# Stick-breaking attention with tokens on the partitions, running sums on VectorE and four panels ahead of each norm

## The chip, the cores and the metric

The kernel runs on one core of a Trainium2 chip. The metric is the device time of one execution in microseconds (us); the time shown is the median of three runs. The engines are named as in the profile: PE is TensorE, DVE VectorE, ACT ScalarE, POOL GpSimd, SP SyncE (here it only issues transfers).

## The reference

One inference step of an encoder with two layers, in fp32, for 256 prompt tokens and 64 tokens of a running stream ("samples"), which the kernel carries together as T = 320 columns. The model dimension is 2048 (16 tiles of 128), the feed-forward one 8192.

```python
# layer 0                                     # layer 1
h = x @ w_in_a                                kv = x @ w_kv; h = x @ w_in_b
main = gate_b * short_conv(gate_c * xin)      main = stick_breaking(q, k, v)        # 12 heads of 128
# both
mix = concat(main, mem_attend(q_m, mem_k, mem_v)) @ w_out     # 4 memory heads, 256 memory tokens
x = layer_norm(ALPHA * x + mix, g0, b0)
x = layer_norm(ALPHA * x + square(relu(x @ w_ff1)) @ w_ff2, g1, b1)
# stick_breaking, strictly causal: keys s before query t
z = q . k / sqrt(128)
A[t, s] = exp(log_sigmoid(z[t, s]) + sum over s < j < t of log_sigmoid(-z[t, j]))
out[t] = sum over s of A[t, s] * v[s]
# mem_k, mem_v = memory tokens @ w_mem_kv, per layer
```

A prompt query sees the prompt's 256 tokens; a sample query sees 512 cached tokens and the 64 new ones.

## The kernel before

Products are kept at fp32 accuracy by splitting: ACT casts a chunk of weights (128x1024, 512 KB from SP's queue) to fp32r, `hi` (L135), DVE subtracts it from the chunk and leaves the rest, `lo` (L136), and `gemm` makes three products per tile of the inner dimension: lo with xh, hi with xl, hi with xh (L181 to L183). Activations lie with the model dimension on the partitions and the 320 tokens as columns. A panel is 256 output columns of weights, two tiles; it has 2 x 16 x 3 = 96 products. Three buffers hold raw chunks, five hi and lo; four PSUM banks (`pacc`) hold accumulators, four more (`paux`: zs, zp, tp, av) all else.

Work between panels is put into the stream of products by hand: `later(gap, fn)` queues a stage, and `tick`, called every 12 products, starts the next one when its gap is over. A scheduler then orders each engine's instructions by when their inputs are ready.

- `mem_kv` projects the memory tokens to keys and values for both layers at the start. It makes layer 0's K and V together, with K's accumulators in `pacc` and V's in `paux`; then layer 1's K and after it layer 1's V (L213 to L215), each in `pacc`. ACT copies finished accumulators to SBUF (L219, L223).
- Layer 1's projection gives for each of the 12 heads kT, qT and vT, a tile of 96 / 2 = 48 products each, so two heads are 288 products. Behind them `stick_z` makes the scores with the keys on the partitions, adds masks by a bf16 product with an identity, and forms softplus(z) by Abs, Exp, Ln on ACT and a maximum and addition on DVE (L626). `sums` adds the suffix sums on PE, as products of a triangle `ntri` with the split softplus (L660 to L665), straight onto the scores in PSUM; ACT's Exp gives the weights, and `values` multiplies them with v (L672 to L681). Sample scores and values are products of half the array's columns (L615, L679, L681).
- `Norm` gathers the residual `res` tile by tile (`add`), subtracts an early estimate of the mean (`center`), sums tiles and squares, and in `finish` gets mean and variance over the partitions by four fp32 products with a matrix of 1/2048 (L411 to L414). The next projection does not wait for it: its first two panels run on the not yet normalised xh, xl with two more columns (322), which carry the weight's sums with gain and bias, and `finished` repairs their results on DVE. `normalise`, called after every chunk step, makes the normalised `res` and its split in turns 2 to 5 (`AFTER`). The last norm writes the output instead (`write`): an addition and a multiplication per tile on DVE or POOL, gain and bias on ACT or DVE, then the transfer.

Of the kernel before, what the change touches and what calls it, by code (L numbers as in the profile page):

```python
# [10 lines left out]
F32 = mybir.dt.float32  # L11
# [6 lines left out]
P = 128  # L18
# [11 lines left out]
CK = 4  # L30
NKC = KT // CK
AFTER = (2, 3, 4, 5)
# [9 lines left out]
def encoder_step(  # L42
# [40 lines left out]
    with tc.tile_pool(name="early", bufs=1) as early:  # L83
# [3 lines left out]
        for _ in range(EARLY):  # L87
# [8 lines left out]
    ident_b = const.tile([P, P], BF16, name="ident_b")  # L96
    nc.vector.tensor_copy(ident_b, ident)

    mask_b = const.tile([P, P], BF16, name="mask_b")
    nc.gpsimd.memset(mask_b, 0.0)  # L100
    nc.gpsimd.affine_select(out=mask_b, in_=mask_b, pattern=[[1, P]], compare_op=ALU.is_gt,
                            fill=BIG, base=0, channel_multiplier=-1)
    ones = const.tile([P, P], F32, name="ones")
    nc.vector.memset(ones, -1.0)
    nones = const.tile([P, P], F32R, name="nones")
    nc.vector.tensor_copy(nones, ones)

    trif = res[:, KT - 1, :P]
    nc.gpsimd.memset(trif, -1.0)
    nc.gpsimd.affine_select(out=trif, in_=trif, pattern=[[-1, P]], compare_op=ALU.is_ge,  # L110
                            fill=0.0, base=0, channel_multiplier=1)
    ntri = const.tile([P, P], F32R, name="ntri")
    nc.vector.tensor_copy(ntri, trif)
    onesm = const.tile([P, P], F32, name="onesm")
    nc.vector.memset(onesm, 1.0 / DM)
    onesq = const.tile([P, P], F32, name="onesq")
    nc.vector.memset(onesq, 1.0 / (4 * P))
# [73 lines left out]
    def mem_kv(layer, whats, between=None, first=None):  # L191

        accs = {}
        for what in whats:
            for i in range(4):
                accs[what, i] = (pacc.tile([P, 512], F32, name="acc") if what == whats[0] else
                                 paux.tile([P, 512], F32, name=("zs", "zp", "tp", "av")[i]))[:, :NM]
        parts = [(what, part) for what in whats for part in range(2)]

        def products(c, what, part, wh, wl, ks):  # L200
            for j in range(2):
                acc = accs[what, 2 * part + j]
                cols = slice(j * P, (j + 1) * P)
                for k in ks:
                    kt = c * CK + k
                    mh, ml = memh[:, kt, :], meml[:, kt, :]
                    start, stop = kt == 0, kt == KT - 1
                    if what == 0:
                        mm(acc, lhsT=wl[:, k, cols], rhs=mh, start=start, stop=False)  # L209
                        mm(acc, lhsT=wh[:, k, cols], rhs=ml, start=False, stop=False)  # L210
                        mm(acc, lhsT=wh[:, k, cols], rhs=mh, start=False, stop=stop)
                    else:
                        mm(acc, lhsT=ml[:, cols], rhs=wh[:, k, :], start=start, stop=False)  # L213
                        mm(acc, lhsT=mh[:, cols], rhs=wl[:, k, :], start=False, stop=False)  # L214
                        mm(acc, lhsT=mh[:, cols], rhs=wh[:, k, :], start=False, stop=stop)  # L215
# [122 lines left out]
    class Norm:  # L338
# [3 lines left out]
        def __init__(self, idx, factor, last=False):  # L342
            self.idx, self.factor, self.last, self.turn = idx, factor, last, 0
            if not last:
# [7 lines left out]
        def ahead(self, m):  # L352
            if self.last:
                return
            r, g, hi = res[:, m, :], lg[:, self.idx, m:m + 1], xh[:, m, :T]
# [4 lines left out]
        def add(self, m, acc):  # L360
# [12 lines left out]
            if not last:  # L373
# [6 lines left out]
        def center(self):  # L380
# [8 lines left out]
            mm(cp, lhsT=onesq, rhs=self.s1, start=True, stop=True)  # L389
            c = work.tile([P, T], F32, name="cen", bufs=1)  # L390
            nc.scalar.copy(c, cp)
# [15 lines left out]

        def finish(self, sq):
            m1 = paux.tile([P, 512], F32, name="zp")[:, :T]
            m2 = paux.tile([P, 512], F32, name="zs")[:, :T]  # L410
            mm(m1, lhsT=onesm, rhs=self.s1, start=True, stop=False)  # L411
            mm(m2, lhsT=onesm, rhs=self.s2, start=True, stop=False)
            mm(m1, lhsT=onesm, rhs=res[:, KT - 1, :], start=False, stop=True)
            mm(m2, lhsT=onesm, rhs=sq, start=False, stop=True)  # L414
            msq = work.tile([P, T], F32, name="msq", bufs=1)
            nc.scalar.activation(msq, m1, AF.Square)
            nc.scalar.mul(mneg, m1, -1.0)
# [10 lines left out]
            if self.last:  # L428
                self.write()

        def write(self):

            for m in range(KT):
                r, g, b = res[:, m, :], lg[:, self.idx, m:m + 1], lb[:, self.idx, m:m + 1]
                engine = nc.gpsimd if m % 3 == 2 else nc.vector
                engine.tensor_tensor(out=r, in0=r, in1=mneg, op=ALU.add)  # L436
                engine.tensor_tensor(out=r, in0=r, in1=rstd, op=ALU.mult)  # L437
                if m % 4 == 3:
                    nc.vector.tensor_scalar(out=r, in0=r, scalar1=g, scalar2=b, op0=ALU.mult, op1=ALU.add)
                else:  # L440
                    nc.scalar.activation(r, r, AF.Identity, bias=b, scale=g)
                if m < 2:
                    nc.sync.dma_start(out=y_out[:, m, :], in_=r)
                elif m % 2:
                    nc.sync.dma_start(out=y_out[:, m - 1:m + 1, :], in_=res[:, m - 1:m + 1, :])

        def normalise(self, _):

            self.turn += 1
            if self.turn not in AFTER:  # L450
                return
            c = AFTER.index(self.turn)
            s = slice(c * CK, (c + 1) * CK)
            r = res[:, s, :]
            nc.vector.tensor_tensor(out=r, in0=r, in1=mneg.unsqueeze(1).to_broadcast([P, CK, T]), op=ALU.add)
            nc.vector.tensor_tensor(out=r, in0=r, in1=rstd.unsqueeze(1).to_broadcast([P, CK, T]), op=ALU.mult)
            for m in range(c * CK, (c + 1) * CK):
                nc.scalar.activation(res[:, m, :], res[:, m, :], AF.Identity, bias=lb[:, self.idx, m:m + 1],
                                     scale=lg[:, self.idx, m:m + 1])
            split(xh[:, s, :T], xl[:, s, :T], r)  # L460
# [18 lines left out]
    def feed_forward(layer, before):  # L479
        for g in range(4):  # L480
# [21 lines left out]
            for p in range(0, 8, 2):  # L502
                first = g == 0 and p == 0
                gemm([[w_ff1[layer, 8 * g + p + i, c] for c in range(NKC)] for i in range(2)], xh, xl,
                     lambda i, j, acc, p=p: hidden(2 * (p + i) + j, acc),
                     width=T + 2 if first else T, after=before.normalise if g == 0 else None)
# [88 lines left out]

    def stick_z(h, d):
        kT, qT = d["kT"], d["qT"]
        ckT = work.tile([P, PAST], F32, name="ckT")
        nc.gpsimd.dma_start(out=ckT, in_=ck[h])

        def z():

            d["zp"] = zp = paux.tile([P, 512], F32, name="zp")[:, :3 * P]
            d["zs"] = zs = paux.tile([P, 512], F32, name="zs")[:, :5 * TS]
            mm(zp[:, 0:P], lhsT=ident_b, rhs=mask_b, start=True, stop=False, **kw)
            mm(zp[:, P:2 * P], lhsT=ident_b, rhs=mask_b, start=False, stop=False, **kw)
            mm(zp[:, 0:P], lhsT=kT[:, 0:P], rhs=qT[:, 0:P], start=False, stop=True, **kw)
            mm(zp[:, P:2 * P], lhsT=kT[:, P:TP], rhs=qT[:, P:TP], start=False, stop=True, **kw)
            mm(zp[:, 2 * P:], lhsT=kT[:, 0:P], rhs=qT[:, P:TP], start=False, stop=True, **kw)
            qs = qT[:, TP:T]  # L610
            mm(zs[:, 4 * TS:], lhsT=ident_b, rhs=mask_b[:, 0:TS], start=True, stop=False, **kw)
            mm(zs[0:TS, 4 * TS:], lhsT=kT[:, TP:T], rhs=qs, start=False, stop=True, **kw)
            for b in range(4):
                for f in range(2):
                    mm(zs[f * 64:(f + 1) * 64, b * TS:(b + 1) * TS], lhsT=ckT[:, b * P + f * 64:b * P + (f + 1) * 64],  # L615
                       rhs=qs, start=False, stop=True, **kw)

            d["npr"] = npr = work.tile([P, 3 * P], F32, name="npr", bufs=1)
# [167 lines left out]
```

## Time and profile before

| | before |
|---|---|
| median of 3 runs (lowest, highest) | 2814.73 us (2813.58, 2815.86) |
| the profiled execution | 2817.14 us, its span 2815.4 us |
| busy PE / DVE / ACT / POOL | 2787.8 / 1427.9 / 1120.1 / 49.2 us |
| bytes moved | 427.52 MB, 152 GB/s over the span |

Busy time of an engine is the time in which it had an instruction running; products on PE overlap, so their pace is better read from the distance between their starts. In the span, memory keys and values take the first 104 us, layer 0 follows with its norms near 511 and 1416, the stick-breaking stage runs from 1418 to 1780, the third norm stands near 1887, and the last ends the run from 2791.

### The profile page before, as it was taken

The numbers are of one execution on the slowest core, as the hardware profiler recorded it, in microseconds if no ns is written. First come the engines' busy times: TensorE is split into PE (matmuls) and PEld (weight loads), VectorE is DVE, ScalarE is ACT, GpSimd is POOL, SyncE is SP. The second block draws the span as 40 slices with busy tenths as digits, with TensorE's granted clock in tenths as the row PEclk, the third lists the DMA queues.
The fourth block names the chain that finished last, engine by engine and source line by source line (L and its number), as shares of the span: only waits on it lengthen the run. The fifth ranks groups of instructions, "written<-read, shape, count | busy, mean of one in ns | idle before, by whom it ended". The sixth has DMA issues, their size and how long they took to land.

```text
span 2815.4 us, 45949 instructions
## 1 busy us (share of the span) xinstructions
PE 2787.8 (99%) x19432; PEld 2765.4 (98%) x19432; DVE 1427.9 (51%) x1913; ACT 1120.1 (40%) x1537; POOL 49.2 (2%) x89
## 2 busy tenths in 40 slices
PE   9999999999999999999999999999999999999996
PEld 9999999999999999999999999999999999999996
DVE  5554457744444344445674444666444444444465
ACT  4433334542333243234454444445323323423333
POOL 1000000000000000000000000000000000000001
PEclk9999999999999999999999999999999999999998
DMA  7645555445554555555545544445555445455542
GB/s 249 217 150 150 150 151 150 142 150 150 150 150 150 150 150 150 150 150 150 150 132 158 154 154 146 129 150 151 150 149 150 151 150 150 150 150 151 150 148 90
DMA packets 119262, 427.52 MB, mean 152 GB/s; under 512 B 13888, under 2 KB 15472, under 8 KB 119056
## 3 DMA queue, kind: packets, MB, share of 16 engines
q1 hardware_dynamic: 115056, 412.14, 48.7%
q0 software_dynamic: 4000, 12.45, 1.3%
q8 instruction: 152, 2.49, 0.4%
q14 instruction: 54, 0.44, 0.0%
HBM read 415.86 MB, written 8.68 MB: 151 GB/s over the span
## 4 chain that ended last, share of the span: by engine, by line
PE 96%; DMA 2%; DVE 1%; ACT 0%; SPq 0%; issue 0%; ACTq 0%; DVEq 0%
PE acc L181 31%; PE acc L183 31%; PE acc L182 31%; DMA raw<-w_mem 2%; DVE lo L136 0%; PE acc L213 0%; PE acc L214 0%; PE acc L215 0%; ACT hi L135 0%; PE av L679 0%; DVE res L437 0%; DVE res L436 0%; PE zs L615 0%; DMA res<-xT 0%; DMA raw<-memT 0%; PE zp L660 0%
## 5 line engine op out<-in xcount | busy, mean ns | idle before, releaser
L136 DVE TENSOR_TENSOR lo<-raw,hi 128x1024 fp32r<-128x1024 f32 (+1 forms) x776 | 940.8, 1214 | 1203.1 <-ACT hi L135 1201.9
L135 ACT CAST hi<-raw 128x1024 fp32r<-128x1024 f32 (+1 forms) x776 | 806.0, 1040 | 1371.6 <-PE acc L183 1285.2
L181 PE MATMUL acc<-xh,lo 128*128 128x320 f32 (+1 forms) x3328 | 1032.3, 310 | 0.0
L183 PE MATMUL acc<-xh,hi 128*128 128x320 f32 (+1 forms) x3328 | 1030.7, 310 | 0.0
L182 PE MATMUL acc<-xl,hi 128*128 128x320 f32 (+1 forms) x3328 | 1027.4, 309 | 0.0
L183 PE MATMUL acc<-mh,hi 128*128 128x320 f32 x2560 | 792.1, 309 | 0.0
L181 PE MATMUL acc<-mh,lo 128*128 128x320 f32 x2560 | 791.3, 309 | 0.0
L182 PE MATMUL acc<-ml,hi 128*128 128x320 f32 x2560 | 791.0, 309 | 0.0
L181 PEld LDWEIGHTS acc<-xh,lo 128*128 128x128 f32 x3328 | 626.5, 188 | 3.5 <-issue 1.5
L183 PEld LDWEIGHTS acc<-xh,hi 128*128 128x128 f32 x3328 | 627.0, 188 | 0.0
L182 PEld LDWEIGHTS acc<-xl,hi 128*128 128x128 f32 x3328 | 625.9, 188 | 0.2
L181 PEld LDWEIGHTS acc<-mh,lo 128*128 128x128 f32 x2560 | 480.5, 188 | 0.4
L183 PEld LDWEIGHTS acc<-mh,hi 128*128 128x128 f32 x2560 | 480.5, 188 | 0.3
L182 PEld LDWEIGHTS acc<-ml,hi 128*128 128x128 f32 x2560 | 480.5, 188 | 0.0
L135 ACT CAST mh<-rs 128x320 fp32r<-128x320 f32 x128 | 58.5, 459 | 53.7 <-DVE rs L492 53.5
L136 DVE TENSOR_TENSOR ml<-rs,mh 128x320 fp32r<-128x320 f32 x128 | 62.3, 488 | 31.7 <-ACT mh L135 31.6
L492 DVE TENSOR_TENSOR rs<-rl 128x320 f32<-128x320 f32 x128 | 62.4, 488 | 8.0 <-ACT rl L490 8.0
L499 DVE SCALAR_TENSOR_TENSOR res<-res,acc 128x320 f32<-128x320 f32 x96 | 46.4, 484 | 39.2 <-PE acc L183 39.2
L490 ACT ACTIVATE rl<-acc 128x320 f32<-128x320 f32 x120 | 52.3, 436 | 33.0 <-PE acc L183 30.7
L372 ACT ACTIVATE sq<-res 128x320 f32<-128x320 f32 x48 | 22.5, 470 | 59.4 <-DVE res L369 59.4
L209 PE MATMUL acc<-memh,lo 128*128 128x256 f32 x128 | 36.9, 288 | 1.2 <-DVE lo L136 1.2
L210 PE MATMUL acc<-meml,hi 128*128 128x256 f32 x128 | 36.2, 283 | 0.0
(251 smaller groups left out, 1191.1 us busy)
## 6 DMA issues: line engine op xcount, KB each, us to landing
raw<-w_ff SPq DMA_DIRECT2D x512, 512.0 KB, 3.6
raw<-w_in_a SPq DMA_DIRECT2D x80, 512.0 KB, 3.6
raw<-w_in_b SPq DMA_DIRECT2D x80, 512.0 KB, 3.6
raw<-w_out SPq DMA_DIRECT2D x64, 512.0 KB, 3.6
raw<-w_mem SPq DMA_DIRECT2D x28, 512.0 KB, 4.6
ckT<-ck POOLq DMA_DIRECT2D x12, 256.0 KB, 3.3
cvS<-cv POOLq DMA_DIRECT2D x12, 256.0 KB, 3.5
res<-xT SPq DMA_DIRECT2D x4, 640.0 KB, 7.5
```

What stands on the lines that cost most here:

```text
L135: nc.scalar.copy(hi, src)
L136: nc.vector.tensor_tensor(out=lo, in0=src, in1=hi.bitcast(F32), op=ALU.subtract)
L181: mm(acc, lhsT=lo[:, k, cols], rhs=ah[:, kt, :width], start=kt == 0, stop=False)
L182: mm(acc, lhsT=hi[:, k, cols], rhs=al[:, kt, :width], start=False, stop=False)
L183: mm(acc, lhsT=hi[:, k, cols], rhs=ah[:, kt, :width], start=False, stop=kt == n * CK - 1)
L209: mm(acc, lhsT=wl[:, k, cols], rhs=mh, start=start, stop=False)
L210: mm(acc, lhsT=wh[:, k, cols], rhs=ml, start=False, stop=False)
L372: nc.scalar.activation(sq, res[:, m, :], AF.Square)
L490: nc.scalar.activation(r, acc, AF.Relu)
L492: nc.vector.tensor_tensor(out=s, in0=r, in1=r, op=ALU.mult)
L499: nc.vector.scalar_tensor_tensor(out=res[:, m, :], in0=res[:, m, :], scalar=ALPHA if g == 0 else 1.0, in1=acc, op0=ALU.mult, op1=ALU.add)
```

## The change

The scores get the query tokens on the partitions (`mm(zp, lhsT=qT, rhs=kT)`), so that the sum over keys runs along the free dimension. The masks are fp32 tiles that DVE adds; the running sum is `tensor_tensor_scan` on DVE, backwards over the keys. The sample scores of an even and an odd head stand on the two halves of one bank's partitions and are worked on together after the odd head. The weights are transposed by PE before they meet v. The triangle, the bf16 identity and the split of the sums go. Besides, `mem_kv` multiplies the low part last and puts V into `paux` in both layers; the three inner norms split their sums and multiply them as fp32r between products of the next projection; four panels instead of two run ahead of each norm, with the split of x in later turns; and the last norm multiplies by the gain early, reads m1 and a copy of rstd from PSUM on DVE, and sends 16 tiles one by one.

```diff
-AFTER = (2, 3, 4, 5)
+AHEAD = 4
...
-                accs[what, i] = (pacc.tile([P, 512], F32, name="acc") if what == whats[0] else
+                accs[what, i] = (pacc.tile([P, 512], F32, name="acc") if what == 0 else
...
-                        mm(acc, lhsT=wl[:, k, cols], rhs=mh, start=start, stop=False)
+                        mm(acc, lhsT=wh[:, k, cols], rhs=mh, start=start, stop=False)
                         mm(acc, lhsT=wh[:, k, cols], rhs=ml, start=False, stop=False)
-                        mm(acc, lhsT=wh[:, k, cols], rhs=mh, start=False, stop=stop)
+                        mm(acc, lhsT=wl[:, k, cols], rhs=mh, start=False, stop=stop)
...
+        def mean(self, out, s, tag):
...
+            split(hi, lo, s)
+            mm(out, lhsT=onesr, rhs=hi, start=True, stop=False)
+            mm(out, lhsT=onesr, rhs=lo, start=False, stop=True)
...
+            else:
+                self.mean(m1, self.s1, "cen")
+                self.mean(m2, self.s2, "r0")
...
+            rstd_p = paux.tile([P, 512], F32, name="av")[:, :T]
+            nc.scalar.copy(rstd_p, rstd)
             for m in range(KT):
                 r, g, b = res[:, m, :], lg[:, self.idx, m:m + 1], lb[:, self.idx, m:m + 1]
-                engine = nc.gpsimd if m % 3 == 2 else nc.vector
-                engine.tensor_tensor(out=r, in0=r, in1=mneg, op=ALU.add)
-                engine.tensor_tensor(out=r, in0=r, in1=rstd, op=ALU.mult)
...
+                    nc.vector.scalar_tensor_tensor(out=r, in0=m1, scalar=self.ng[:, m:m + 1], in1=r,
+                                                   op0=ALU.mult, op1=ALU.add)
...
+                if m % 8 in (3, 5, 7):
+                    nc.vector.tensor_tensor(out=r, in0=r, in1=rstd_p, op=ALU.mult)
+                else:
+                    nc.gpsimd.tensor_tensor(out=r, in0=r, in1=rstd, op=ALU.mult)
...
-                if g == 0 and m < 4:
+                if g == 0 and m < 2 * AHEAD:
...
+    def before_tokens(n):
+
+        w = n.shape[1]
+        nc.vector.tensor_tensor_scan(out=n[:, ::-1], data0=one.to_broadcast([P, w]), data1=n[:, ::-1], initial=0.0,
+                                     op0=ALU.mult, op1=ALU.add)
...
+            mm(zp[:, 0:P], lhsT=qT[:, 0:P], rhs=kT[:, 0:P], start=True, stop=True, **kw)
+            mm(zp[:, P:3 * P], lhsT=qT[:, P:TP], rhs=kT[:, 0:TP], start=False, stop=True, **kw)
...
+            if h % 2:
+
+                zs = paux.tile([P, PAST], F32, name="zs")
+                for i, e in enumerate(heads):
+                    half = slice(i * TS, (i + 1) * TS)
+                    mm(zs[half, :], lhsT=e["qT"][:, TP:T], rhs=e["ckT"], start=True, stop=True, **kw)
...
+            nc.vector.scalar_tensor_tensor(out=n, in0=ap, scalar=0.0, in1=n, op0=ALU.max, op1=ALU.add)
+            before_tokens(n[:, 0:P])
+            before_tokens(n[:, P:3 * P])
+            nc.vector.tensor_tensor(out=ap, in0=ap, in1=n, op=ALU.subtract)
+            nc.scalar.activation(ap, ap, AF.Exp)
...
+                before_tokens(ns)
+                nc.vector.tensor_tensor(out=as_[:, :PAST], in0=zs, in1=ns[:, :PAST], op=ALU.subtract)
+                nc.vector.tensor_tensor(out=own, in0=own, in1=ns[:, PAST:], op=ALU.subtract)
+                nc.scalar.activation(as_, as_, AF.Exp)
...
+            for b in range(3):
+                nc.tensor.transpose(at[:, b, :], d["ap"][:, b * P:(b + 1) * P], ident)
+            if h % 2:
+                st = paux.tile([P, 4, P], F32, name="zs")
+                for b in range(4):
+                    nc.tensor.transpose(st[:, b, :], d["as"][:, b * P:(b + 1) * P], ident)
+                nc.tensor.transpose(at[:TS, 3, :], d["as"][:, PAST:], ident)
...
-            for part in ("npl", "nph"):
-                mm(zp, lhsT=ntri, rhs=d[part], start=False, stop=False, **kw)
-            mm(zp[:, 2 * P:], lhsT=ones, rhs=npr[:, P:2 * P], start=False, stop=True, **kw)
...
+            mm(o[:, 0:TP], lhsT=vS[:, 0, :], rhs=aT[:, 0:TP], start=True, stop=False, **kw)
+            mm(o[:, P:TP], lhsT=vS[:, 1, :], rhs=aT[:, TP:], start=False, stop=True, **kw)
...
-        later(1, turn)
-        later(1, sums)
-        later(2, values)
+        later(1, turn, 5)
...
+             width=T + 2 if p < AHEAD else T, after=after if p <= AHEAD else None)
```

On PE, in the middle of the stick-breaking stage, before: the sums of one head (zp its prompt scores, zs its sample scores) and then its values stand in the stream of the projection.

```order
L660 MATMUL zp<-npl,ntri 128x384
L660 MATMUL zp<-nph,ntri 128x384
L661 MATMUL zp<-npr,ones 128x128
L663 MATMUL zs<-nsl,ntri 128x320
L663 MATMUL zs<-nsh,ntri 128x320
L665 MATMUL zs<-nsl,nones 128x256
L665 MATMUL zs<-nsh,nones 128x256
...
L672 MATMUL av<-npr,vS 128x128
L673 MATMUL av<-npr,vS 128x128
L674 MATMUL av<-npr,vS 128x128
L679 MATMUL av<-nsm,cvS 64x64 x8
L681 MATMUL av<-nsm,vS 64x64 x2
```

The same place now, of an odd head: values of the even head, scores of the odd one, the sample scores of both, 48 products of the projection, transposes of v and of the prompt weights, 12 products, transposes of the sample weights, 48 products, and with the next head's scores the sample values of the pair.

```order
L722 MATMUL av<-aT,vS 128x256
L723 MATMUL av<-aT,vS 128x128
L643 MATMUL zp<-kT,qT 128x128
L644 MATMUL zp<-kT,qT 128x256
L652 MATMUL zs<-ckT,qT 64x512 x2
L655 MATMUL zp<-kT,qT 64x64 x2
...
L702 MATMUL zp<-ident,npr 128x128 x3
...
L706 MATMUL zs<-ident,nsm 128x128 x4
L707 MATMUL zp<-ident,nsm 64x128
...
L737 MATMUL av<-asT,cvS 64x64 x8
```

The sums moved off PE, and L706 and L707, which have the sample weights to wait for, came into its stream 60 products behind the scores. On DVE, between the odd head's scores and L706, there stands now (the rows printed as SCALAR_TENSOR_TENSOR at L627 are the scans):

```order
L660 TENSOR_TENSOR npr<-zp,mask_p 128x384
L673 TENSOR_TENSOR nsm<-zp,mask_s 128x64
L664 SCALAR_TENSOR_TENSOR a<-npr,a 128x384
L627 SCALAR_TENSOR_TENSOR a<-one,a 128x128
L627 SCALAR_TENSOR_TENSOR a<-one,a 128x256
L679 SCALAR_TENSOR_TENSOR ns<-zs,ns 128x512
L667 TENSOR_TENSOR npr<-npr,a 128x384
L679 SCALAR_TENSOR_TENSOR ns<-nsm,ns 128x64
L134 TENSOR_TENSOR lo<-raw,hi 128x1024
L627 SCALAR_TENSOR_TENSOR ns<-one,ns 128x576
L709 COPY vS<-tp 128x256
L681 TENSOR_TENSOR nsm<-zs,ns 128x512
```

Three scans came into DVE's part of the chain, and a cast of a weight chunk stands between them. At a norm, PE had the four sums between the last product of one projection and the first of the next:

```order
L183 MATMUL acc<-mh,hi 128x320
L411 MATMUL zp<-s_4294,onesm 128x320
L412 MATMUL zs<-s_4295,onesm 128x320
L413 MATMUL zp<-res,onesm 128x320
L414 MATMUL zs<-sq,onesm 128x320
L181 MATMUL acc<-xh,lo 128x322
```

Now the next projection begins at once, and the split sums follow after 17, 24, 26 and 27 of its products:

```order
L416 MATMUL zp<-sh,onesr 128x320
L181 MATMUL acc<-xh,hi 128x322
...
L416 MATMUL zs<-sh,onesr 128x320
L179 MATMUL acc<-xh,lo 128x322
L180 MATMUL acc<-xl,hi 128x322
L417 MATMUL zp<-sl,onesr 128x320
L181 MATMUL acc<-xh,hi 128x322
L417 MATMUL zs<-sl,onesr 128x320
```

The sums moved from the gap between two projections into the second one's first panels.

## Rows read from the trace of the kernel before

**Rows 1.** Windows: PE, PEld, DVE, ACT, POOL busy us (count), granted clock, DMA share.

```profile
80.00:100.00 20.00, 20.00 (x158) 20.00 (x157) 9.37 (x9) 8.84 (x10) 1.79 (x4) 0.92 0.83 297
514.00:541.00 27.00, 27.00 (x183) 27.00 (x182) 25.87 (x26) 21.09 (x34) 0.00 (x0) 1.00 0.38 117
600.00:1300.00 700.00, 700.00 (x4776) 700.00 (x4776) 308.87 (x348) 247.17 (x300) 0.00 (x0) 1.00 0.50 150
...
1420.00:1480.00 60.00, 60.00 (x417) 57.03 (x415) 49.03 (x73) 34.92 (x66) 2.33 (x5) 1.00 0.43 133
1480.00:1790.00 310.00, 310.00 (x2474) 302.43 (x2470) 134.07 (x208) 143.86 (x238) 23.66 (x44) 1.00 0.49 150
```

**Rows 2.** Waits of PE over the whole run: us, times, longest.

```profile
PE acc L213 <- ACT mk_sb L219: 1.9, 1, 1.9
```

**Rows 3.** The chain that ended last, two heads apart: start, us, engine, tile, line.

```profile
1507.62 0.47 PE zs L615 x15
...
1559.97 0.47 PE zs L615 x15
```

**Rows 4.** Timeline of PE, memory attention of layer 1: start, us, line, operation.

```profile
1448.46 1.02 PE L294 MATMUL zs<-mk_sb,fin 128*128 128x256 f32 x4
1449.32 1.03 PE L294 MATMUL zp<-mk_sb,fin 128*128 128x256 f32 x4
1450.28 0.65 PE L299 MATMUL tp<-smk,fin 128*64 128x256 f32 x4
1450.86 0.42 PE L181 MATMUL acc<-xh,lo 128*128 128x320 f32 x1
```

**Rows 5.** Timeline of PE, two transposes of a head's v.

```profile
1593.75 0.27 PE L649 MATMUL tp<-ident,vT 128*128 128x128 f32 x1
1593.86 0.27 PE L650 MATMUL tp<-ident,vT 128*128 128x128 f32 x1
```

**Rows 6.** Timeline of PE, sample values of the same head.

```profile
1601.22 0.69 PE L679 MATMUL av<-nsm,cvS 128*64 128x64 f32 x16
1601.83 0.33 PE L681 MATMUL av<-nsm,vS 64*64 64x64 f32 x4
1602.09 0.42 PE L181 MATMUL acc<-xh,lo 128*128 128x320 f32 x1
```

**Rows 7.** Timeline of PE, sums of the first norm and the products after them.

```profile
511.19 0.81 PE L411 MATMUL zp<-s,onesm 128*128 128x320 f32 x2
...
513.78 0.31 PE L182 MATMUL acc<-xl,hi 128*128 128x322 f32 x1
```

**Rows 8.** Timeline of ACT at the start, memory layer 1.

```profile
90.15 2.94 ACT L135 CAST hi<-raw 128x1024 fp32r<-128x1024 f32 x3
```

**Rows 9.** Timeline of DVE at the same place.

```profile
91.69 3.49 DVE L136 TENSOR_TENSOR lo<-raw,hi 128x1024 fp32r<-128x1024 f32 x3
```

**Rows 10.** Groups of DVE by shape: busy us, mean ns, idle before.

```profile
L136 DVE TENSOR_TENSOR lo<-raw,hi 128x1024 fp32r<-128x1024 f32 x764 | 934.7, 1225 | 1200.0 <-ACT hi L135 1199.1
...
L136 DVE TENSOR_TENSOR nsl<-nsm,nsh 128x576 fp32r<-128x576 f32 x12 | 9.1, 755 | 5.2 <-ACT nsh L135 5.2
```

**Rows 11.** Timeline of POOL in the tail, first of two groups.

```profile
2793.66 5.12 POOL L436 TENSOR_TENSOR res<-res,mneg 128x320 f32<-128x320 f32 x5 [1024.10 <-ACT mneg L417]
```

**Rows 12.** Timeline of DVE in the tail.

```profile
2793.42 0.49 DVE L420 SCALAR_TENSOR_TENSOR var<-zs,msq 128x320 f32<-128x320 f32 x1 [1.73 <-PE zs L414]
...
2796.92 1.14 DVE L425 SCALAR_TENSOR_TENSOR msq<-r 128x320 f32<-128x320 f32 x1
...
2799.45 0.48 DVE L436 TENSOR_TENSOR res<-res,mneg 128x320 f32<-128x320 f32 x1
2799.85 0.48 DVE L427 SCALAR_TENSOR_TENSOR rstd<-var,r 128x320 f32<-128x320 f32 x1
...
2811.59 0.45 DVE L439 TENSOR_SCALAR res<-res,lgb 128x320 f32<-128x320 f32 x1
```

More of the change, by code (lines that the diff above doesn't have):

```diff
@@ L372, in add @@
             nc.scalar.activation(sq, res[:, m, :], AF.Square)
-            if not last:
+            if not (last and self.last):
                 nc.vector.tensor_tensor(out=self.s1, in0=self.s1, in1=res[:, m, :], op=ALU.add)
@@ L440, in write @@
                 else:
                     nc.scalar.activation(r, r, AF.Identity, bias=b, scale=g)
[L442 to L447, printed above, removed]
-            self.turn += 1
[L450 to L460, printed above, removed]
+                nc.sync.dma_start(out=y_out[:, m, :], in_=r)
@@ new lines, in normalise, with some @@
+        def normalise(self, turn):
+            self.turn += 1
+            def some(first):
+                c = self.turn - first
+                return slice(c * CK, (c + 1) * CK) if 0 <= c < NKC else None
+            s = some(2)
+            if s:
+                r = res[:, s, :]
+                nc.vector.tensor_tensor(out=r, in0=r, in1=mneg.unsqueeze(1).to_broadcast([P, CK, T]), op=ALU.add)
+                nc.vector.tensor_tensor(out=r, in0=r, in1=rstd.unsqueeze(1).to_broadcast([P, CK, T]), op=ALU.mult)
+                for m in range(s.start, s.stop):
+                    nc.scalar.activation(res[:, m, :], res[:, m, :], AF.Identity, bias=lb[:, self.idx, m:m + 1],
+                                         scale=lg[:, self.idx, m:m + 1])
+            s = some(turn)
+            if s:
+                split(xh[:, s, :T], xl[:, s, :T], res[:, s, :])
@@ L609, in z @@
[L609 to L616, printed above, removed]
@@ new lines, in z @@
+            if done and h % 2 == 0:
+                done[1]()
+            if h % 2:
[3 more added lines that the diff above has]
+                    mm(zs[half, :], lhsT=e["qT"][:, TP:T], rhs=e["ckT"], start=True, stop=True, **kw)
+                for i, e in enumerate(heads):
+                    half = slice(i * TS, (i + 1) * TS)
+                    mm(zp[half, 3 * P:3 * P + TS], lhsT=e["qT"][:, TP:T], rhs=e["kT"][:, TP:T], start=False, stop=True,
+                       **kw)
@@ new lines, in z @@
+            d["ap"] = ap = work.tile([P, 3 * P], F32, name="npr", bufs=1)
+            n = work.tile([P, 3 * P], F32, name="a")
+            nc.vector.tensor_tensor(out=ap, in0=zp[:, :3 * P], in1=mask_p.rearrange("p a b -> p (a b)"), op=ALU.add)
+            nc.scalar.activation(n, ap, AF.Abs)
+            nc.scalar.activation(n, n, AF.Exp, scale=-1.0)
+            nc.scalar.activation(n, n, AF.Ln, bias=1.0)
+            nc.vector.scalar_tensor_tensor(out=n, in0=ap, scalar=0.0, in1=n, op0=ALU.max, op1=ALU.add)
@@ new lines, in sample @@
+        def sample():
+            o = d["o"]
+            for i, e in ((1, d), (0, even)):
+                cols = slice(TP, T) if i else slice(T, T + TS)
+                for b in range(5):
+                    for f in range(2):
+                        half = slice(f * 64, (f + 1) * 64)
+                        keys = P if b < 4 else TS
+                        values_ = e["cvS"][:, b, half] if b < 4 else e["vS"][:TS, 2, half]
+                        mm(o[half, cols], lhsT=values_, rhs=d["asT"][:keys, b, i * TS:(i + 1) * TS], start=False,
+                           stop=b == 4, **kw)
```

185 lines of the change are left out of this document (96 added, 89 removed).

## Prediction

> **What bounds the kernel now.** I read the windows first [rows 1]: in 600 to 1300 us TensorE (PE) is busy for all 700.00 us with 4776 products, 146.6 ns each, while DVE has 309 and ACT 247 us of work. In the stick-breaking stage (1480 to 1790) it is the same picture: PE 310 of 310 us, DVE 134, ACT 144. Then the waits of PE [rows 2]: the longest in the whole run is 1.9 us, at the first V product of memory layer 1 (L213), for the copies that free its accumulators. So the kernel is a solid line of PE work with a short start and a tail, and a change pays by what it takes off PE or off the tail; work added to DVE or ACT costs only where it makes PE wait.
>
> **What the change does, part by part.** The sum is made against the profiled execution, 2817.1 us (2.4 above the median of 2814.73); each term is a difference in us.
>
> *D, stick-breaking on PE.* The chain passes the burst of products of L615 at 1507.62 and again, two heads later, at 1559.97 [rows 3]: 52.35 us for two heads. A pair has 288 products of the projection; at 146.6 ns they are 42.2, so 10.1 us go to attention. What will they be after? Four fp32 products of 128x256 (L294, two passes each, so x4 is two products) begin at 1448.46 and 1449.32 [rows 4]: 0.43 us for 256 columns, so 0.22 for 128. A head's scores z are 256 + 128 columns (L643, L644), its values the same (L722, L723): 4 x 0.65 = 2.6 a pair. The sample scores of two heads stand on two halves of the array's columns (L652, 2 x 512 columns). L299 is such a pair at 256 columns: 0.58 us from 1450.28 to the next product [rows 4], against 0.43 for one full product and 0.86 for two, so halves run side by side with 0.15 for going in and out; at 512 columns 0.86 + 0.15, and about 0.2 more for the small pair of L655 and its switch: 1.2. A transpose starts 0.11 us after the one before [rows 5]; there are 17 a pair (6 of v, 6 of prompt weights, 5 of sample weights): 1.9. Sample values keep their form; eight half products took 0.61, two 0.26 [rows 6], two heads 1.75. With 0.3 for switches the pair is 7.7 instead of 10.1; six pairs give **-14**. Bounds: if the halves of L652 and L655 ran one after the other, +0.8 a pair, so -9; with nothing for switches -16. Gone are the mask products, the running sums (L660 to L665) and the 64-column score products.
>
> *E, the chain off PE that now feeds PE.* In the order of an odd head PE has 60 projection products and six transposes from the end of z to L706, 9.4 us; L706 needs the sample weights. Behind z stand, on DVE and ACT by turns: mask added, Abs, Exp, Ln, max-and-add, three scans (L627; 128, 256, 576 elements), subtraction, Exp, and between them casts of weight chunks. An ordinary DVE pass takes 0.755 us at 576 elements and 1.225 at 1024 [rows 10], 1.05 ns an element; consecutive passes start 0.08 closer than they are long (0.40 for 0.48 at 2799.45 and 2799.85 [rows 12]). With these I laid the rows of the order one behind the other: with scans as ordinary passes L706's data are ready some 9.0 us after z, no wait. A scan is not in this trace. Below it is bounded by the ordinary pass, above by the slowest elementwise row, POOL's 5.12 us for five of 320 [rows 11], 3.2 ns an element; that makes the chain 1.7 to 2 us longer, a wait of 1.3 to 1.6 at L706. I take the middle, 2.1 ns: 576 in 1.36 us, chain 9.8 to 9.9, a wait of 0.48. Behind L706 on PE stand the projection's products, so the wait is lost in full: 6 x 0.48 = **+2.9** (0 to +9). Even heads have 120 products of cover. [...]
>
> *B, norms.* The four fp32 sums L411 to L414 and the first product behind them take from 511.19 to 513.78 [rows 7], less one product 2.44 us; three norms do so. After, four fp32r products (0.59) inside the stream, whose inputs are cast while 17 to 24 projection products run, with 0.2 for their weights: 3 x (2.44 - 0.79) = **-5.0** (-5.5 to -3, if a product waits for its cast).
>
> *C, four panels with 322 columns:* 576 more such products. In 514 to 541 one takes 147.5 ns against 146.6 [rows 1]: **+0.6** (up to +2).
>
> *A, start.* V's accumulators of layer 1 come from other banks, so the 1.9 us wait [rows 2] goes. [...] That the low part's product now comes last counts at nothing. Against it: PE arrives 2 us earlier at the second V chunk, whose cast stands behind a cast of x: its hi cast begins at 90.15 [rows 8], its lo at 91.69 [rows 9] and ends at 92.9, where PE would ask at about 91.5: a wait of some 1.3 and perhaps the lower clock after it. Best case -3.5, with wait and clock again -0.9; I take **-2.3** (-0.5 to -4).
>
> *F, tail.* Before, the last DVE operation ends at 2812.04 [rows 12], 3.4 us before the span's end: copy out and closing. DVE and POOL run additions together, and DVE's take 1.14 at 2796.92 where it needs 0.48 alone at 2799.45 [rows 12]; rstd is ready at 2800.3. After, POOL has nothing until rstd, which moves to about 2797.1. DVE then has 17 operations at 0.41 with one input in PSUM: 2804.1. POOL has ten multiplications, between 0.40 (DVE's pace) and 1.02 each [rows 11]; its first of five, when DVE was not yet in its way, is the nearest: about 0.8, so 2805.3. ACT adds 16 biases at about 0.5: 2806.3 or so. With 3.4 behind them the end is at 2809.9 in place of 2815.4: **-5.5** (-4 to -6.5). That DVE is free of POOL rests on L420, one input in PSUM, 0.49 us [rows 12] with POOL starting at 2793.66 [rows 11] inside it. [...] By the row of 1.14 for each of DVE's operations beside POOL, the tail would gain 0.9 instead.
>
> *G, DVE around norms.* In 1420 to 1480 DVE is busy 49.0 of 60 us [rows 1], and gets two more panels of finishing and the new sums there; splits of x come later but, by the order, before the panel that reads them. Weight casts are two chunks ahead: **+0.3** (0 to +4).
>
> Sum: -14 - 5.0 + 0.6 - 2.3 + 2.9 - 5.5 + 0.3 = -23.0: 2794.1 for a profiled execution, on the median 2814.73 - 23.0 = **2791.7**.
>
> **Rivals.**
> 1. *The scans are dear, and PE waits at L706 of every odd head.* At POOL's rate the term is about +9 instead of +2.9: 2798. To end on the other side (slower than before) the wait must exceed (23.0 + 2.9) / 6 = 4.3 us a head, so the 960 scanned elements must cost 4.8 ns each above an ordinary pass, 5.9 in all. For: each element depends on the one before, and nothing here shows such an operation. Against: no DVE row is near, even POOL's is at 3.2.
> 2. *Column halves run one after the other* where both read 512 columns: D is -9, 2796.7. For: L299's pair has 256 columns only; against: its 0.58 us.
> 3. *The tail collides as before:* F is -0.9, 2796.3.
> 4. *The start only moves its wait and the clock falls again, and DVE's bunching behind norms makes PE wait:* A -0.5, G +4: 2797.2.
> 5. *The gain in D is smaller or undone, since the stage's limit is elsewhere,* as if DVE or ACT were the bound of the stage: 134 and 144 of 310 us speak against it; without D's 14 the time is 2806.
>
> **How the numbers follow.** Forecast 0.55; rival 1 0.15 (of which 0.03 slower than before), 2 0.08, 3 0.07, 4 0.10, 5 0.05. Cases 1 to 4 lie at 2796 to 2798, two of them together at about 2802; the lower end takes the better bounds of D, A and F, -8 together: 2783. Range 2783 to 2803. Faster by over 0.2% (5.6 us, about what a measurement of this kernel can tell from no change) 0.95, within it 0.02, slower 0.03.
>
> **What would show it.** D: the chain's bursts of two heads 49.5 to 50.5 us apart. E: waits of PE at L706, six of 0.5 us, for ACT's asT or as; the scan's own row, 1.36 at 576. B: no gap and no fp32 product at 511, L416 and L417 between projection products. A: no wait at 77, a shorter one near 91, the clock of 80 to 100. F: rstd at 2797, DVE rows at 0.41 to 0.49 beside POOL, a last output at about 2806. The prediction is wrong if PE waits over 2 us in any odd head, or if the pair's period stays above 51.5.

## The result and the profile after

The changed kernel takes 2797.44 us (median of 6 runs, 2797.0 to 2800.08) against 2815.10 of before in the same job (2813.58 to 2815.86, 6 runs): ratio 0.9939, 95% interval 0.9928 to 0.995, 17.7 us less. The range 2783 to 2803 holds it; the forecast of 2791.7 lies 5.7 too low. The profiled executions are 20.1 apart (2817.14 and 2797.00; spans 2815.4 and 2795.2): that of before stood 2.0 above its median, that of after 0.4 below, so 2.5 us of the miss lie between the two profiled executions and the medians. What made them differ from the others no trace shows. The rest is sought in the stretches of the two traces, cut at products that both programs have. "First product with xh" is at 104.03 before and 99.94 after, the last product of the stream at 2790.85 and 2773.71.

| stretch, by the starts of products | before | after | difference | terms, as forecast |
|---|---|---|---|---|
| start to the first product with xh | 104.03 | 99.94 | -4.1 | A -2.3 |
| norm 0: last product before it to the last with xh after it | 115.47 | 114.33 | -1.1 | a third of B and C: -1.5 |
| norm 1 to the last product with mh before norm 2 | 470.77 | 460.01 | -10.8 | D, E, G, a third of B and C: -12.3 |
| norm 2, as norm 0 | 115.47 | 114.33 | -1.1 | a third of B and C: -1.5 |
| last product of the stream to the span's end | 24.59 | 21.51 | -3.1 | F -5.5 |

The other stretches agree to 0.01 us, and the five differences add up to the 20.2 us between the two spans. The waits of PE after (line waited for: us in total, times, longest) answer to [rows 2]:

```profile
PE zs L706 <- ACT nsm L683: 2.7, 5, 0.5
PE av L88 <- DVE filled L85: 1.5, 1, 1.5
PE acc L207 <- ACT hi L133: 1.1, 1, 1.1
PE acc L209 <- DVE lo L134: 0.8, 2, 0.6
```

The wait for K's copies is gone; the wait of the forecast at L706 is there, five times and not six. Windows of after, against [rows 1]:

```profile
80.00:100.00 20.00, 20.00 (x168) 19.92 (x167) 9.96 (x9) 9.88 (x13) 1.61 (x3) 1.00 0.84 296
1480.00:1790.00 310.00, 307.13 (x2251) 294.87 (x2250) 162.93 (x242) 141.57 (x223) 23.23 (x43) 1.00 0.51 154
```

The granted clock of 80 to 100 us is 1.00 (it was 0.92, with 158 products instead of 168), and no wait stands near 91 us. In the stick-breaking stage DVE has 29 us more work, and PE 2.9 us of idle time. One odd head's burst on PE, and its transposes (timeline):

```profile
1546.93 0.60 PE L722 MATMUL av<-aT,vS 128*128 128x256 f32 x2
1547.37 0.38 PE L723 MATMUL av<-aT,vS 128*128 128x128 f32 x2
1547.59 0.39 PE L643 MATMUL zp<-kT,qT 128*128 128x128 f32 x2
1547.81 0.60 PE L644 MATMUL zp<-kT,qT 128*128 128x256 f32 x2
1548.34 1.08 PE L652 MATMUL zs<-ckT,qT 128*64 128x512 f32 x4
1549.24 0.28 PE L655 MATMUL zp<-kT,qT 128*64 128x64 f32 x4
1549.46 0.42 PE L179 MATMUL acc<-xh,lo 128*128 128x320 f32 x1
...
1559.70 0.66 PE L706 MATMUL zs<-ident,nsm 128*128 128x128 f32 x4 [0.54 <-ACT nsm L683]
1560.20 0.27 PE L707 MATMUL zp<-ident,nsm 128*64 128x128 f32 x1
```

L652 begins at 1548.34 and L655 0.90 us later: two times 512 columns in little more than one full product of that width (0.86 by [rows 4]), so the halves do run side by side, and rival 2 falls. The chain passes the sample values once per pair (start, us):

```profile
1568.84 1.75 PE av L737 x40
1619.60 1.75 PE av L737 x40
```

They are 50.76 us apart for two heads, against 52.35 [rows 3]: 1.6 less, with a wait of 0.54 in it. The prediction had named 49.5 to 50.5. These are the scans in the chain that PE waits for, on DVE (groups by shape; busy us, mean ns):

```profile
L627 DVE TENSOR_TENSOR_SCAN ns<-one,ns 128x576 f32<-128x576 f32 x6 | 8.1, 1354 | 0.0
L627 DVE TENSOR_TENSOR_SCAN a<-one,a 128x256 f32<-128x256 f32 x12 | 8.0, 666 | 0.0
L627 DVE TENSOR_TENSOR_SCAN a<-one,a 128x128 f32<-128x128 f32 x12 | 5.0, 421 | 0.2
```

From 128 to 576 elements a scan grows by 933 ns, 2.08 ns an element, twice what the forecast took for an ordinary pass from [rows 10]; for a scan it took 2.1.

### The profile page after: what moved, and what is told of

Same layout as the page of the kernel before. It is cut to its first block, busy times and chain, and to the rows that moved or that the text cites. A ratio compares the mean times of both kernels' runs of the same rounds, so it can differ in the third digit from the quotient of the medians.

```text
span 2795.2 us, 45378 instructions
## 1 busy us (share of the span) xinstructions
PE 2769.9 (99%) x19138; PEld 2746.0 (98%) x19138; DVE 1453.6 (52%) x1961; ACT 1126.5 (40%) x1552; POOL 47.8 (2%) x91
## 4 chain that ended last, share of the span: by engine, by line
PE 96%; DVE 2%; ACT 1%; DMA 0%; issue 0%; POOL 0%; SPq 0%; POOLq 0%; ACTq 0%
PE acc L179 30%; PE acc L181 30%; PE acc L180 30%; DVE lo L134 1%; PE acc L209 1%; PE acc L207 0%; PE acc L208 0%; PE av L737 0%; ACT hi L133 0%; DMA raw<-w_mem 0%; DVE ns L627 0%; DVE a L627 0%; POOL res L462 0%; SPq L141 0%; ACT nsm L683 0%
## 5 line engine op out<-in xcount | busy, mean ns | idle before, releaser
L207 PE MATMUL acc<-memh,hi 128*128 128x256 f32 x128 | 36.6, 286 | 1.1 <-ACT hi L133 1.1
```

What stands on the lines that cost most here:

```text
L207: mm(acc, lhsT=wh[:, k, cols], rhs=mh, start=start, stop=False)
```

## The experiments

All are edits of the changed kernel, so the number to compare with is 2797.44. They ran in three jobs, in which the kernel before had medians of 2815.13, 2815.81 and 2814.79 (2815.10 above), so a difference of medians between jobs can be off by some 0.7; the second job held the old stick-breaking, the old sums, the old banks and the two panels. Theory: each part of the change acts in its own stretch and the parts add; the scan's price makes PE wait; the tail is short of its forecast since POOL's last operations end too late.

**The wait at L706: more cover.**

```diff
-        later(1, turn, 5)
+        later(1, turn, 7)
```

> The changed kernel, but the transposes of the weights are started two ticks (24 products) later. Main theory (the 0.5 us waits of PE at L706, 2.7 us in all, are lost in full and only 0.5 us of cover is missing): these waits vanish, none takes their place, 2.7 us less than the changed kernel, about 2794.7 us. Rival (the cover is only moved: the copies of the transposed weights now come late, 36 products before the values instead of 48): waits appear at L722 or L737 instead, time within 0.7 us of 2797.4.

It took 2793.12 us (2792.58 to 2793.97), 4.3 less than the changed kernel. The waits that are left (us in total, times, longest):

```profile
PE av L88 <- DVE filled L85: 1.5, 1, 1.5
PE acc L209 <- DVE lo L134: 0.8, 3, 0.3
PE acc L207 <- ACT hi L133: 0.8, 1, 0.8
```

There is no wait at L706, and none in its place at L722 or L737: the rival falls. The stretch from norm 1 to norm 2 is 3.8 us shorter than in the changed kernel, 1.1 more than the waits; two heads are 50.01 us apart, 0.75 less. The next run shows where most of the difference lies.

**The scan's price: an ordinary pass in its place** (the running sums are left out).

```diff
-        nc.vector.tensor_tensor_scan(out=n[:, ::-1], data0=one.to_broadcast([P, w]), data1=n[:, ::-1], initial=0.0,
-                                     op0=ALU.mult, op1=ALU.add)
+        nc.vector.tensor_tensor(out=n[:, ::-1], in0=n[:, ::-1], in1=n[:, ::-1], op=ALU.max)
```

> The changed kernel with an ordinary elementwise pass of the same shapes in place of the three running sums, which are left out. Main theory (a running sum costs about 2.1 ns an element, twice an ordinary pass, and that is what makes PE wait): the passes take about 0.29, 0.42 and 0.76 us instead of 0.42, 0.67 and 1.35, the chain to L706 is 1.0 us shorter, no wait at L706, about 2794.7 us. Rival (the chain is late because of ACT's passes and the weight casts between them, the sums hardly matter): waits at L706 of 0.3 us or more stay, over 2796 us.

It took 2793.45 us (2792.62 to 2793.93), 4.0 less. The passes (mean ns in the last column but one):

```profile
L627 DVE TENSOR_TENSOR a<-a 128x256 f32<-128x256 f32 x12 | 5.0, 418 | 0.0
L627 DVE TENSOR_TENSOR ns<-ns 128x576 f32<-128x576 f32 x6 | 4.5, 752 | 0.0
L627 DVE TENSOR_TENSOR a<-a 128x128 f32<-128x128 f32 x12 | 3.5, 288 | 0.2
```

There is no wait at L706's place, as the forecast worked out from [rows 10] for an ordinary pass; the wait is the scans' doing. Two heads are 50.10 us apart, with PE's order unchanged: 0.66 less than with the scans, where the wait's own row says 0.54. The 12 products before L706 take 1.88 us from their first start to L706's here, 2.55 in the changed kernel. So a wait at this place costs 0.12 more than its row says, and the stretch from norm 1 to norm 2, again 3.8 us shorter, is the better measure of what the scans cost. The later transposes save another 0.09 a pair, standing in one burst.

**The scan's price: one more of 384 elements** in each odd head's chain.

```diff
+                spare = work.tile([P, 3 * P], F32, name="a")
+                nc.vector.tensor_tensor_scan(out=spare[:, ::-1], data0=one.to_broadcast([P, 3 * P]),
+                                             data1=ns[:, 3 * P - 1::-1], initial=0.0, op0=ALU.mult, op1=ALU.add)
                 before_tokens(ns)
```

> The changed kernel with one more running sum of 384 elements in each odd head's chain, into a spare tile, so that the outputs stay the same; L706 stands three products later than in the changed kernel. Main theory (every us of that chain beyond its cover is a us of PE): the extra sum takes 0.95 us, less 0.44 of cover it adds 0.5 to each wait: waits of about 1.05 us, 3 us more in all, about 2800.4 us. Rival (slack elsewhere takes it up): waits below 0.8 us and less than 1 us more.

It took 2799.58 us (2798.86 to 2799.75), 2.1 more, with this wait (L709 is L706 of the others):

```profile
PE zs L709 <- ACT nsm L686: 5.5, 6, 0.9
```

There are six waits of 0.9 us, 2.8 us more in all; expected were 1.05 and 3. The stretch from norm 1 to norm 2 is 2.7 us longer than in the changed kernel, so the time follows the waits: the chain beyond its cover is paid in full, and no slack takes it up.

**The tail: seven multiplications on POOL instead of ten.**

```diff
-                if m % 8 in (3, 5, 7):
+                if m in (3, 5, 7, 9, 11) or m > 11:
```

> The changed kernel with seven instead of ten of the last multiplications on POOL, none of them after tile 10; DVE makes the other nine. Main theory (the end of the run waits for POOL: its last operation ends at 2788.7 and the span ends 6.5 us later, while in the kernel before the span ended 3.4 us after the last DVE operation): POOL ends 2.5 us earlier, then the last outputs bound, the span's end is about 1.9 us earlier, about 2795.5 us. Rival (the closing takes 4.8 us after ACT's last operation whatever POOL does): ACT ends about 0.6 us earlier and so does the span, about 2796.8 us.

It took 2794.28 us (2793.36 to 2794.62), 3.2 less; from the last product of the stream to the span's end 19.1 us instead of 21.5. POOL's and ACT's last groups in the changed kernel (timeline; span 2795.2):

```profile
2780.49 8.23 POOL L462 TENSOR_TENSOR res<-res,rstd 128x320 f32<-128x320 f32 x10 [1029.03 <-DVE rstd L443]
...
2789.75 0.64 ACT L466 ACTIVATE res<-res,lgb 128x320 f32<-128x320 f32 x1
```

and with seven on POOL (span 2792.8):

```profile
2780.41 5.78 POOL L462 TENSOR_TENSOR res<-res,rstd 128x320 f32<-128x320 f32 x7 [1029.00 <-DVE rstd L443]
...
2788.97 0.65 ACT L466 ACTIVATE res<-res,lgb 128x320 f32<-128x320 f32 x1
```

Counted from the last product of the stream, ACT ends 0.7 us earlier, the span 2.4. The span ends 6.5 and 6.6 us after POOL's last operation.

**The tail: four on POOL** (one run).

```diff
-                if m % 8 in (3, 5, 7):
+                if m == 3 or m > 4:
```

> The changed kernel with only four of the last multiplications on POOL. Main theory (the span ends 6.5 us after POOL's last operation or some 3 us after ACT's last one, whichever is later): POOL ends near 2784, 10 us before the end, and no longer matters; DVE's three more operations make the last output 1.2 us later than with seven on POOL, so 20.3 us from the last product of the stream to the span's end, against 19.1 with seven and 21.5 with ten. Rival (each operation taken off POOL shortens the end): under 18.5 us.

It took 2796.17 us; its tail is 20.0 us (span 2794.5):

```profile
2781.24 3.32 POOL L462 TENSOR_TENSOR res<-res,rstd 128x320 f32<-128x320 f32 x4 [1029.01 <-DVE rstd L443]
...
2791.00 0.65 ACT L466 ACTIVATE res<-res,lgb 128x320 f32<-128x320 f32 x1 [0.30 <-DVE res L460]
```

POOL ends 9.9 us before the end and no longer decides; the span ends 2.8 us after ACT's last operation, which waited for DVE. So two limits cross near seven, and the rival (each operation off POOL helps) falls. The traces also hold the engines' closing instructions, and these show which limit it is. POOL closes with a drain that is over 5.7 us after its last operation in all four kernels: at 2794.44 with ten multiplications, 2791.91 with seven, 2790.29 with four, and 2811.43 before the change. SP's closing, which with ten and before the change is over 0.3 and 0.2 us behind the landing of the last output, is over at 2792.54, 2792.00, 2793.71 and 2814.68. The span ends 0.8 us after the later of the two: that is POOL's with ten, SP's by 0.1 with seven, and SP's with four and before the change.

**The old stick-breaking in the changed kernel** (`stick_z`, `stick_a` and their constants as before).

```diff
-    def before_tokens(n):
...
+            for part in ("npl", "nph"):
+                mm(zp, lhsT=ntri, rhs=d[part], start=False, stop=False, **kw)
...
+        later(1, turn)
+        later(1, sums)
+        later(2, values)
```

> The changed kernel with the stick-breaking of before (keys on the partitions, triangle sums on PE, samples of one head at a time). Main theory (the parts add up, and the new stick-breaking is worth the 9.6 us by which the two traces differ between norm 1 and norm 2 when the norm's own share is taken off, its 2.7 us of waits included): about 2807 us, two heads 52.35 us apart again, no wait at L706's place. Rival (the gain of that stage came from the norm and the four panels): under 2802 us.

It took 2806.09 us (2805.72 to 2808.62), 8.7 more. Two heads on the chain:

```profile
1503.27 0.47 PE zs L647 x15
...
1555.63 0.47 PE zs L647 x15
```

They are 52.36 us apart, as before the change; the stretch from norm 1 to norm 2 is 9.7 us longer than in the changed kernel. The new stick-breaking is worth 9.7 us by the traces with its waits (8.7 by the medians), and 3.8 more without them. The profiled execution is 11.6 us longer than the changed kernel's, since its first product with xh also starts 2.0 later.

**The old sums of the norms.**

```diff
-            if self.last:
-                mm(m1, lhsT=onesm, rhs=self.s1, start=True, stop=False)
...
-            else:
-                self.mean(m1, self.s1, "cen")
-                self.mean(m2, self.s2, "r0")
+            mm(m1, lhsT=onesm, rhs=self.s1, start=True, stop=False)
+            mm(m2, lhsT=onesm, rhs=self.s2, start=True, stop=False)
+            mm(m1, lhsT=onesm, rhs=res[:, KT - 1, :], start=False, stop=True)
+            mm(m2, lhsT=onesm, rhs=sq, start=False, stop=True)
```

> The changed kernel with the four fp32 sums of before in the gap between the projections, for all norms; four panels ahead stay. Main theory (the sums inside the stream save the 2.2 us gap and cost 0.6 to 0.9, three times): 4 to 5 us more than the changed kernel, about 2802 us, with a gap of 2.36 us at each inner norm. Rival (moving the sums only moved the time): under 2799 us.

It took 2802.19 us (2801.6 to 2802.83), 4.8 more. Norm 0:

```profile
508.14 0.31 PE L181 MATMUL acc<-mh,hi 128*128 128x320 f32 x1
508.30 0.81 PE L422 MATMUL zp<-s,onesm 128*128 128x320 f32 x2
...
510.50 0.55 PE L179 MATMUL acc<-xh,lo 128*128 128x322 f32 x1
```

The gap of 2.36 us is back. From the last product before norm 0 to the last with xh behind it there are 115.89 us here, 114.33 in the changed kernel and 115.47 in the kernel before: the sums in the stream save 1.56 a norm, the two more wide panels cost 0.42. Three times 1.56 are 4.7; the medians differ by 4.8, the profiled executions by 5.8, of which 1.2 stand at the start.

**V's old banks in memory layer 1.**

```diff
-                accs[what, i] = (pacc.tile([P, 512], F32, name="acc") if what == 0 else
+                accs[what, i] = (pacc.tile([P, 512], F32, name="acc") if what == whats[0] else
```

> The changed kernel with V's accumulators of memory layer 1 back in the banks that K has just used; the new order of the three products stays. Main theory (the start's 4.1 us are the wait for K's copies, 2.1 us of PE, and the granted clock that fell to 0.92 over 80 to 100 us behind it): the wait at V's first product is back at about 2 us, the clock of that stretch is below 1 again, 3 to 4 us more, about 2801 us. Rival (the order of the products did it): within 1 us of 2797.4.

It took 2801.69 us (2800.32 to 2802.09), 4.3 more. The wait of PE, and the window:

```profile
PE acc L211 <- ACT mk_sb L217: 2.3, 1, 2.3
```

```profile
80.00:100.00 20.00, 19.52 (x150) 19.52 (x151) 9.05 (x9) 8.49 (x12) 2.15 (x4) 0.91 0.77 276
```

Wait and lower clock are back together, 150 products instead of 168 in that window. In this trace the first product with xh starts at 105.1, 5.2 later than in the changed kernel; 1.2 of that are a wait for a cast near 75 us, of a kind that the run without scans shows too (0.9).

**The old order of the three products in the memory projections** (one run).

```diff
-                        mm(acc, lhsT=wh[:, k, cols], rhs=mh, start=start, stop=False)
+                        mm(acc, lhsT=wl[:, k, cols], rhs=mh, start=start, stop=False)
```

> The changed kernel with the old order of the three products in the memory projections (the low part first); V's new banks stay. Main theory (the order is worth next to nothing, the banks did it): the first product with xh within 1 us of the changed kernel's 99.9 us, no wait at V's first product. Rival (the low part in last place hides the casts): later by 1.5 us or more, with waits for the low part at the first V or K products.

It took 2796.86 us; the first product with xh starts at 99.86 us (99.94 in the changed kernel). The order is worth nothing here; the banks did it.

**Two panels ahead instead of four.**

```diff
-AHEAD = 4
+AHEAD = 2
...
-                     width=T + 2 if first else T, after=(lambda _: before.normalise(NKC + 2)) if g == 0 else None)
+                     width=T + 2 if first else T, after=(lambda _: before.normalise(2)) if g == 0 else None)
...
-    after = lambda _: norm.normalise(2 * NKC + 2)
+    after = lambda _: norm.normalise(2)
```

> The changed kernel with two panels ahead of each norm instead of four; the sums stay inside the stream and the splits of x come in turns 2 to 5 as before. First theory (four panels are not needed: rstd is ready 12 us behind the first product instead of 6.6, and the splits of x, which before stood 14 to 25 us behind it, still come before the 28 us at which the third panel asks): no wait of PE at the third panel, 384 columns pairs fewer per norm, 0.5 to 1.5 us less than the changed kernel. Rival (the later sums do need the cover): PE waits at the third panel's first products, 2 us or more in all at the three norms, over 2798.5 us.

It took 2802.01 us (2800.55 to 2803.16), 4.6 more: my first theory falls. The waits of PE that are new:

```profile
PE acc L179 <- DVE lo L134: 1.7, 3, 0.7
...
PE acc L179 <- ACT rl L516: 1.3, 2, 0.6
PE zs L292 <- DVE ml L134: 1.2, 1, 1.2
PE zs L308 <- DVE p L283: 0.5, 1, 0.5
```

The reason is not quite the rival's either. PE does not wait for the split of x (xl): it waits for weight casts (lo) and small passes that stand behind the splits on DVE, which in 514 to 541 us is busy 26.45 of 27 us (25.34 in the changed kernel). The wait of PE that ends at 544.38 us is for the first of the two casts in the last row:

```profile
540.90 1.49 DVE L134 TENSOR_TENSOR xl<-res,xh 128x1280 fp32r<-128x1280 f32 x1
542.30 0.89 DVE L134 TENSOR_TENSOR ml<-rs,mh 128x320 fp32r<-128x320 f32 x2
543.10 2.36 DVE L134 TENSOR_TENSOR lo<-raw,hi 128x1024 fp32r<-128x1024 f32 x2
```

The stretch at each of norms 0 and 2 is 1.3 us longer than with four panels, that of norm 1 3.3. Four panels cost PE 0.42 a norm and give DVE the time for its work.

**Both gains together:** `later(1, turn, 7)` and seven multiplications on POOL.

> The changed kernel with the transposes two ticks later and with seven multiplications on POOL in the tail. Main theory (the two gains lie in different stretches and add, 3.7 and 2.4 us by the traces): 2.4 to 3.2 us below the run with the later transposes alone, about 2790.3 us, no wait at L706, 19.1 us from the last product of the stream to the span's end. Rival (one of the two was the noise of a run): over 2792 us.

It took 2790.85 us (2790.28 to 2791.45): ratio to before 0.9914, interval 0.9901 to 0.9928, 6.6 below the changed kernel. Two heads are 50.01 us apart, no wait at L706, the tail is 19.1 us. The gains add as the traces have them, 3.8 and 2.4; the two gains as the medians have them, 4.3 and 3.2, would have made 7.5.

## Why the prediction held, and where its sizes were off

*What bounds the kernel:* right. Every term that the runs undid moved the time by what it moved PE or the ends of the run. On the traces the sum missed by 2.8 us, and its misses do not all go one way: D, E, B, C and F came out 0.6, 0.9, 0.3, 0.7 and 2.4 worse than forecast, A and G 1.8 and 0.3 better.

*D, stick-breaking, -14: measured -13.4* (the stretch's -10.8, less the norm's -1.1, with the 3.8 taken off that the scans cost). The side-by-side halves came as priced from L299: 0.90 for the wide pair, where 0.86 + 0.15 was taken. Without scans a pair has 7.9 us beside its projection products (50.10 - 42.22); forecast were 7.7.

*E, the wait at L706, +2.9: measured +2.7 by the waits' rows, +3.8 by what the stretch gains without them.* The middle between an ordinary pass and POOL's rate was a choice between two bounds, and that it met the price of a scan, 2.08 ns an element, was luck. The term was too small since a wait takes 0.66 from the stream and not 0.48. From 128 to 576 elements the scans grow by 2.08 ns an element, the ordinary passes of the same shapes in the run without scans by 1.04 (288 to 752 ns): a scan's element takes twice the time here.

*B, -5.0, and C, +0.6: measured -4.7 and +1.3.* The wide products cost 2.2 ns more each, not the 0.9 of the window taken: its count of 183 holds products that only overlap its edges, and by their starts the wide ones stand 148.8 ns apart.

*A, -2.3: measured -4.1.* The best case of the sum, -3.5, is the 1.9 us of the wait [rows 2] and 1.6 us for the clock, as much as 0.92 in place of 1.00 makes over the 20 us of its row [rows 1]. Both parts came. In the kernel before, the wait for K's copies held PE up by 2.1 us from start to start (77.18 to 79.41, less the 0.12 of one product), and behind it the granted clock was 0.50:

```profile
79.60:83.00 3.40, 3.40 (x17) 3.40 (x17) 2.18 (x2) 1.62 (x4) 2.14 (x4) 0.50 0.73 194
```

The 48 products from 79.41 us on took 7.34 us, where 48 take 5.76 at a clock of 1.00: 1.6 us. The wait of 1.3 us near 91 us, which the middle value allowed for, did not come, and the best case, -3.5, was passed, since a wait of 0.4 us for a cast near 74 us fell away too. In this run the transfer of x let ACT begin its cast at 87.46 instead of 88.98, and the casts of V's chunks behind it came 1.5 us earlier as well. Ten traces have the new banks and the low part last. In those where the cast of x began by 87.9 us PE did not wait for V's low part; where it began at 88.3 it waited 0.5 us, at 88.7 and 89.4 (old sums, old stick-breaking) 1.2 us, and the first product with xh came at 100.8, 101.1 and 101.9. So the wait depends on when x arrives, and that A beat its middle value was luck; why x arrives when it does was not settled.

*F, -5.5: measured -3.1, outside its bounds of -4 to -6.5. This is the step that failed:* "With 3.4 behind them the end is at 2809.9". The engines came near to what was forecast: POOL took 0.82 us a multiplication, rstd was ready 2.9 us earlier counted from the last product, DVE's operations with one input in PSUM took 0.48 to 0.55 beside it, where L425, with both inputs in SBUF, took 1.14 beside POOL in the kernel before [rows 12]. Counted from the last product POOL ended at 15.0 us (forecast 14.5) and ACT at 16.7 (15.5). But the 3.4 us were read from a kernel in which POOL had been done for 9.7 us at the span's end. After the change POOL works nearly to the last, and the span ends 6.5 us after its last operation, 5.7 of them in its drain. The forecast's own end of POOL, 2805.3, with 6.5 behind it gives -3.6; the rest is that POOL ended later than forecast. The two runs with seven and four on POOL show its closing as the term that was missing.

*G, +0.3:* nothing is seen in the changed kernel, no wait of PE around the norms. But the run with two panels shows how near it was. The doubt was in the right place, and the four panels, which the sum has as a cost only, are what kept the wait away.

Of the rivals none came true. The first came nearest: PE does wait at L706 for the scans, at 3.8 us and not 9, and to end slower than before it needed 5.9 ns an element.

## What to carry to other kernels

On a kernel whose matrix engine never rests, price a change by the starts of its products in a stretch, and look for the one chain that begins to feed it: work moved to another engine was free here up to the cover that the stream left (no wait with 24 products more), and paid in full beyond it (one more scan made the waits 2.8 us longer and the stretch 2.7), so that starting the consumer two steps later was worth 4 us. Read the closing of each engine that will work in a tail: here the span ended 3.4 us after DVE's last operation where POOL had been done for 9.7 us, and 6.5 us after POOL's where POOL worked nearly to the last, and the first figure did not give the second. A part that looks like a cost (two more wide panels, 0.42 us a norm) may be what makes another part (later sums) affordable, as here, where two panels took 4.6 us more: undo them one by one before calling either superfluous.

## What was not expected of the hardware

The span ended 6.50 to 6.58 us after POOL's last operation in the eleven programs where POOL made seven or ten multiplications at the end, but 2.8 us after ACT's last operation where POOL had ended 9.9 us before. POOL's drain is what takes the time: it was over 5.7 us after POOL's last operation with ten, seven and four multiplications and in the kernel before. After the waits of PE of 1.9 and 2.3 us near 79 us (the kernel before, V's old banks) the granted clock of 80 to 100 us was 0.92 and 0.91; without such a wait it was 1.00 in the changed kernel and in the runs with both gains, two panels, the old order, the old sums and the old stick-breaking, in the last two also behind their waits of 1.2 us near 93 us. What the clock cost behind the wait in the kernel before was 1.6 us (7.34 us for 48 products, against 5.76), nearly as much as the wait itself.
